# Windowed attention in a two-layer decoder trunk: scores of one head over its own 64 rows, and bias, maximum and sink in one VectorE instruction

## The chip, the cores and the metric

The kernel runs on one core of one Trainium2 chip. The metric is the time of one execution on the device, in microseconds (us), as the median of several runs; the runs before the change gave 1440.52 to 1442.91 us, median 1440.92. A profile of one execution comes with it. In it PE is TensorE's matrix multiplication, PEld its weight load, DVE is VectorE, ACT is ScalarE, POOL is GpSimd and SP is SyncE, which issues most of the DMAs.

## The reference: what is computed

The program is a small decoder trunk over 512 tokens of width 1024, with two layers. Layer one mixes the tokens by a gated delta rule, layer two by causal attention in a sliding window of 128 tokens; each is followed by a gated MLP with a short convolution. The change touches the attention alone:

```python
SWA_Q_HEADS = 16
SWA_KV_HEADS = 4
SWA_HEAD_DIM = 64
SWA_WINDOW = 128
SWA_BLOCK = 128

def sliding_window_sink_attention(hn, k, v, w_q, sinks, w_o, bias, mask):
    bsz, t, _ = hn.shape
    nb = t // SWA_BLOCK
    q = (hn @ w_q).reshape(bsz, nb, SWA_BLOCK, SWA_KV_HEADS, SWA_GROUP, SWA_HEAD_DIM)
    q = q * (SWA_HEAD_DIM ** -0.5)
    ...
    kb, vb = band(k), band(v)
    s = jnp.einsum('bnqhgd,bnkhd->bnhgqk', q, kb).astype(jnp.float32) + bias
    s = jnp.where(mask[None, :, None, None], s, NEG_INF)
    sink = sinks.astype(jnp.float32).reshape(SWA_KV_HEADS, SWA_GROUP)[:, :, None]
    m = jnp.maximum(jnp.max(s, axis=-1), sink)
    p = jnp.exp(s - m[..., None])
    denom = jnp.sum(p, axis=-1) + jnp.exp(sink - m)
    probs = (p / denom[..., None]).astype(vb.dtype)
    o = jnp.einsum('bnhgqk,bnkhd->bnqhgd', probs, vb)
    return o.reshape(bsz, t, SWA_Q_HEADS * SWA_HEAD_DIM) @ w_o
```

`band` gives each block of 128 queries its own 128 keys and the 128 before them (block 0 has only its own). There are 16 query heads of 64 features and 4 heads of keys and values, so four query heads share one key head. `bias` depends only on the distance of query and key, `sinks` holds one number per head.

## The kernel before

The program runs one stage after another: the delta rule, its output projection, `ffn(0)`, `attention`, `ffn(1)`. Activations lie with features on the 128 partitions and the 512 tokens along the free dimension; the residual stream `hT` is eight tiles of 128x512. A product of full accuracy is made of three products in a shorter float format: both operands are split into a high and a low part, and high by high, high by low and low by high are added up. `mm3` (lines 145 to 147) does this for a projection: 8 tiles of weights by 3 products, 24 matmuls of 512 columns into one bank `d`; `cast` (lines 129 and 130) splits the weights, the high part on ScalarE, the low one on VectorE; `split` (lines 150 and 151) does the same for activations.

`attention` normalises `hT`, projects keys and values once (`w_kv`), and then goes through the 16 query heads in eight pairs, `p` = 0 to 7. A pair fills 128 partitions: head `j` = 0 on partitions 0 to 63, head `j` = 1 on 64 to 127. Both heads of a pair use the same key head `g = p // 2`. `query(p)` loads the pair's bias rows and projects its queries; it is called two pairs ahead. `attend(p)` works through four blocks `n` of 128 queries. For a block:

- Lines 1161 to 1163: three score products over all 128 rows. So that the heads stay apart, the keys stand in `kbh` and `kbl` as two halves of 512 columns each: half `j` has the keys on head `j`'s 64 rows and zeros on the other 64. One product gives the scores of both heads, 2 x 256 columns (2 x 128 in block 0), in one bank of tag `s`. There are two such banks.
- Lines 1166 to 1171, VectorE: the bias is added while the scores leave the bank for a row `e` of tag `dt`, the maximum over each head's keys is taken, the sink is brought in (`ngm`, the negative maximum), and the sink's exponent is formed.
- Lines 1172 to 1176: exponentials on ScalarE, which also sums them (`den`); the sum and its reciprocal on VectorE.
- Lines 1178 to 1181: scaling by the reciprocal, head 0 on VectorE, head 1 on ScalarE.
- Lines 1186 to 1197: four transposes on TensorE into a bank of tag `g` (two banks), a copy to the row `pT` on ScalarE, and the product with the values, 64 output partitions for each head, into the bank `p`.

At the end of a pair the bank `p` is split into high and low part, which the output projection over `w_o` reads.

The order of instructions on each engine is set before the run by a scheduler that follows the program's order as priority and puts instructions of other parts where it expects an engine to wait. So projections for later queries stand between the scores and the transposes of a pair. On the chip each engine works through its own list in that order, held by semaphores.

Of the kernel before, what the change touches and what calls it, by code (L numbers as in the profile page):

```python
# [8 lines left out]
F32 = mybir.dt.float32  # L9
# [3 lines left out]
ALU = mybir.AluOpType  # L13
# [28 lines left out]
def kernel(  # L42
# [1059 lines left out]
    def attention(h):  # L1102
        toep = rb[:]
        kbh = [wide("G") for g in range(4)]
        kbl = [wide("L") for g in range(4)]
        for a, b in zip(kbh, kbl):
            for t in (a, b):
                G.memset(t[0:64, 1, :].bitcast(F32), 0.0)
                G.memset(t[64:128, 0, :].bitcast(F32), 0.0)
        kxh, kxl = normed(h, NKV)  # L1110
        rs = rstd_rows(h)
        for kv in range(2):
            st = load_stage(w_kv, 0, 8, 256 * kv)
            for i in range(2):
# [4 lines left out]
                if kv == 0:  # L1119
                    for j in range(2):  # L1120
                        g = 2 * i + j
                        src = f[64 * j : 64 * j + 64, :]
                        near, far = (slice(0, 64), slice(64, 128)) if j == 0 else (slice(64, 128), slice(0, 64))
                        hn_, hf_ = kbh[g][near, j, :], kbh[g][far, 1 - j, :]
                        S.copy(hn_, src)
                        S.copy(hf_, src)
                        V.tensor_tensor(kbl[g][near, j, :], src, hn_.bitcast(F32), op=ALU.subtract)
                        V.tensor_tensor(kbl[g][far, 1 - j, :], src, hn_.bitcast(F32), op=ALU.subtract)
# [22 lines left out]

        def attend(p, qh, ql, b3):
            g = p // 2
            po = bank("p")
            for n in range(NC):
                ns = slice(n * P, (n + 1) * P)
                k0 = max(n - 1, 0) * P
                W = (n + 1) * P - k0
                sc = bank("s")
                s3 = sc[:, 0 : 2 * W].rearrange("p (j k) -> p j k", j=2)  # L1160
                PE.matmul(s3, qh[:, ns], kbh[g][:, :, k0 : k0 + W], start=True, stop=False)
                PE.matmul(s3, qh[:, ns], kbl[g][:, :, k0 : k0 + W], start=False, stop=False)
                PE.matmul(s3, ql[:, ns], kbh[g][:, :, k0 : k0 + W], start=False, stop=True)
                e = r2("ga")
                e3 = e[:, 0 : 2 * W].rearrange("p (j k) -> p j k", j=2)
                V.tensor_tensor(e3, s3, b3[:, :, W - 1 :: -1], op=ALU.add)
                sm = cp.tile([P, 8], F32, tag="sm", bufs=6, name=nm("sm"))
                mx, ngm, den, es = sm[:, 0:2], sm[:, 2:4], sm[:, 4:6], sm[:, 6:8]
                V.tensor_reduce(mx, e3, axis=AX.X, op=ALU.max)
                V.scalar_tensor_tensor(ngm, mx, -1.0, nsink[:, 2 * p : 2 * p + 2], op0=ALU.mult, op1=ALU.min)  # L1170
                V.tensor_tensor(es, sink[:, 2 * p : 2 * p + 2], ngm, op=ALU.add)
                S.activation(es, es, AF.Exp)
                for j in range(2):
                    S.activation(e3[:, j, :], e3[:, j, :], AF.Exp, bias=ngm[:, j : j + 1], accum_out=den[:, j : j + 1])  # L1174
                V.tensor_tensor(den, den, es, op=ALU.add)
                V.reciprocal(den, den)
                for j in range(2):
                    if j == 1:
                        S.activation(e3[:, j, :], e3[:, j, :], AF.Copy, scale=den[:, j : j + 1])
                    else:  # L1180
                        V.tensor_scalar(e3[:, j, :], e3[:, j, :], den[:, j : j + 1], None, op0=ALU.mult)
                pt = bank("g")
                nt = 2 * W // P
                for b in range(nt):
                    bs = slice(b * P, (b + 1) * P)
                    PE.transpose(pt[:, bs], e[:, bs], ident[:])  # L1186
# [89 lines left out]
```

## Time and profile before

| | value |
|---|---|
| median of three runs | 1440.92 us |
| the profiled execution: its own time | 1439.8 us |
| its span, first to last instruction | 1438.0 us |
| mean granted TensorE clock | 0.996 |
| key and value projections, TensorE | from about 897 us |
| first score matmul to last value product | 934 to 1032 us |
| matmul records of scores (L1161 to L1163) | 96 |
| records of transposes (L1186) | 112 |
| records of value products (L1191), two for each matmul | 224 |

The profile names work by line, engine, operation and tiles as `out<-in`, with the buffer numbers left out. A mean in nanoseconds is the duration of one instruction. Matmuls are pipelined: a record's duration holds the way through the array, and the distance from one start to the next tells what a matmul keeps from its successors. "128\*64" behind a matmul is the part of the array that it uses, rows by columns. The idle time in brackets behind a row names what the engine waited for.

### The profile page before, as it was taken

Reading aid. Unit: us, or ns where it says so; the run is one execution under the profiler, and the core shown is the slowest. Engines: PE = TensorE matmul, PEld = TensorE weight load, DVE = VectorE, ACT = ScalarE, POOL = GpSimd, SP = SyncE. Lnnn points to the kernel's source line nnn. Section 1 sums busy time; section 2 is a strip of 40 time slices with the busy share of each in tenths; the row PEclk is TensorE's granted clock in tenths of the full one; section 3 lists DMA queues with packets and bytes.
Section 4 is the critical chain, followed back from the end, with each engine's and each line's share of the span. In section 5 each row is a group of like instructions: output and inputs, shape, how many; then the busy total and the mean of one; then the engine's idle time right before and its main releaser. Section 6 shows DMA issues by size and latency. Waiting matters only on the chain.

```text
span 1438.0 us, 21635 instructions
## 1 busy us (share of the span) xinstructions
PE 1401.4 (97%) x8266; PEld 1165.2 (81%) x8266; DVE 1120.6 (78%) x2056; ACT 770.8 (54%) x1518; POOL 20.0 (1%) x47
## 2 busy tenths in 40 slices
PE   7999999999999999999999999999999999999998
PEld 5777878878876888888988888777788888988887
DVE  5896887979764538889968889787757888977896
ACT  7764666666555434444335445588745444344443
POOL 1000000000000000000000002000000000000000
PEclk9999999999999999999999999999999999999999
DMA  5334254264367323321333223311132322332222
GB/s 156 88 106 114 78 174 121 76 182 125 103 220 227 125 88 110 104 74 53 123 124 111 74 81 111 111 59 45 59 108 90 118 81 66 112 123 88 96 70 77
DMA packets 163084, 152.85 MB, mean 106 GB/s; under 512 B 24164, under 2 KB 150693, under 8 KB 162981
## 3 DMA queue, kind: packets, MB, share of 16 engines
q1 hardware_dynamic: 160722, 151.27, 33.3%
q8 instruction: 65, 1.06, 0.3%
q10 hardware_dynamic: 2259, 0.20, 0.2%
q14 instruction: 38, 0.31, 0.1%
HBM read 134.65 MB, written 16.80 MB: 105 GB/s over the span
## 4 chain that ended last, share of the span: by engine, by line
PE 83%; DVE 8%; DMA 6%; ACT 2%; issue 1%; SPq 0%; DVEq 0%; ACTq 0%
PE d L145 21%; PE d L147 20%; PE d L146 20%; DVE wlo L130 2%; PE s L588 1%; PE p L1191 1%; DMA ol<-od 1%; PE d L992 1%; PE g L1186 1%; PE s L603 1%; PE s L628 1%; PE d L990 1%; PE s L992 1%; PE d L991 1%; DMA stage<-in_a_w_in_dram 1%
## 5 line engine op out<-in xcount | busy, mean ns | idle before, releaser
L145 PE MATMUL d<-xh,whi 128*128 128x512 f32 x1192 | 475.2, 400 | 2.9 <-ACT whi L129 2.8
L146 PE MATMUL d<-xl,whi 128*128 128x512 f32 x1192 | 472.8, 398 | 0.0
L147 PE MATMUL d<-xh,wlo 128*128 128x512 f32 x1192 | 472.0, 398 | 0.7 <-DVE wlo L130 0.7
L129 ACT CAST whi<-stage 128x1024 fp32r<-128x1024 f32 (+2 forms) x236 | 229.1, 976 | 230.3 <-PE d L146 153.9
L130 DVE TENSOR_TENSOR wlo<-stage,whi 128x1024 fp32r<-128x1024 f32 (+2 forms) x236 | 265.5, 1129 | 69.2 <-ACT whi L129 68.6
L145 PEld LDWEIGHTS d<-xh,whi 128*128 128x128 f32 x1192 | 224.6, 188 | 51.2 <-ACT whi L129 3.4
L147 PEld LDWEIGHTS d<-xh,wlo 128*128 128x128 f32 x1192 | 224.3, 188 | 51.5 <-DVE wlo L130 2.1
L146 PEld LDWEIGHTS d<-xl,whi 128*128 128x128 f32 x1192 | 224.3, 188 | 46.2 <-issue 1.0
L237 DVE SCALAR_TENSOR_TENSOR acc<-d,cwc,acc 128x511 f32<-128x511 f32 (+2 forms) x96 | 70.7, 739 | 8.3 <-ACT acc L234 7.9
L851 DVE TENSOR_TENSOR sz<-d,p6s 128x512 f32<-128x512 f32 x58 | 39.9, 689 | 40.9 <-PE d L147 38.4
L873 ACT ACTIVATE dt<-dt 128x512 f32<-128x512 f32 x44 | 27.8, 632 | 81.7 <-DVE dt L856 81.7
L856 DVE SCALAR_TENSOR_TENSOR va<-sz,fcw,va 128x511 f32<-128x511 f32 (+1 forms) x58 | 43.4, 747 | 1.8 <-ACT va L854 0.9
L856 DVE SCALAR_TENSOR_TENSOR dt<-sz,fcw,dt 128x511 f32<-128x511 f32 (+1 forms) x58 | 43.3, 746 | 0.9
L511 DVE TENSOR_TENSOR p6s<-sN,sT 64x31 f32<-64x31 f32 (+15 forms) x124 | 40.7, 328 | 2.5 <-DMA sN<-nd 0.5
L517 DVE TENSOR_TENSOR sT<-sT,p6s 64x31 f32<-64x31 f32 (+15 forms) x124 | 41.0, 330 | 1.9
L129 ACT CAST whi<-st 128x768 fp32r<-128x768 f32 (+1 forms) x30 | 23.7, 791 | 30.5 <-DMA st<-in_ffn_w_down_dram 5.6
L851 DVE TENSOR_TENSOR zl<-d,p6s 128x512 f32<-128x512 f32 x30 | 20.7, 689 | 24.0 <-PE d L147 23.3
L636 ACT ACTIVATE rq<-o 128x128 f32<-128x128 f32 x64 | 19.0, 298 | 28.4 <-DVE o L631 15.8
L1174 ACT ACTIVATE dt<-dt,sm 128x256 f32<-128x256 f32 (+1 forms) x64 | 30.3, 474 | 6.7 <-DVE sm L1170 6.6
L875 DVE TENSOR_TENSOR va<-dt,va 128x512 f32<-128x512 f32 x44 | 30.4, 691 | 1.2
L130 DVE TENSOR_TENSOR wlo<-st,whi 128x768 fp32r<-128x768 f32 (+1 forms) x30 | 26.8, 898 | 1.9 <-ACT whi L129 1.8
L854 ACT ACTIVATE dt<-sz,normc,fcw 128x512 f32<-128x512 f32 x29 | 23.7, 817 | 5.2 <-DVE sz L851 5.1
(745 smaller groups left out, 2796.5 us busy)
## 6 DMA issues: line engine op xcount, KB each, us to landing
stage<-in_ffn_w_up_dram SPq DMA_DIRECT2D x44, 1024.0 KB, 5.2
stage<-in_a_w_in_dram SPq DMA_DIRECT2D x23, 1024.0 KB, 5.8
stage<-in_ffn_w_down_dram SPq DMA_DIRECT2D x16, 768.0 KB, 4.7
stage<-in_a_w_out_dram SPq DMA_DIRECT2D x8, 1024.0 KB, 5.5
st<-in_ffn_w_down_dram SPq DMA_DIRECT2D x8, 768.0 KB, 5.8
zd<-sz SPq DMA_DIRECT2D x16, 256.0 KB, 2.0
od<-o SPq DMA_DIRECT2D x16, 256.0 KB, 2.5
stage<-in_b_w_q_dram SPq DMA_DIRECT2D x4, 1024.0 KB, 5.0
```

The source lines that it names most:

```text
L129: S.copy(hi[:, :kt, :m], src)
L130: V.tensor_tensor(lo[:, :kt, :m], src, hi[:, :kt, :m].bitcast(F32), op=ALU.subtract)
L145: PE.matmul(ps, hi[:, k, :m], xh[k], start=first and k == 0, stop=False)
L146: PE.matmul(ps, hi[:, k, :m], xl[k][:], start=False, stop=False)
L147: PE.matmul(ps, lo[:, k, :m], xh[k], start=False, stop=last and k == kt - 1)
L237: V.scalar_tensor_tensor(acc[:, d:], ps[:, : T - d], col, acc[:, d:], op0=ALU.mult, op1=ALU.add)
L511: V.tensor_tensor(tv, N[:, s, s + 1 : 32].unsqueeze(2).to_broadcast([64, n, m]), Tm[:, s : s + 1, 0:m].to_broadcast([64, n, m]), op=ALU.mult,)
L517: V.tensor_tensor(Tm[:, s + 1 : 32, 0:m], Tm[:, s + 1 : 32, 0:m], tv, op=ALU.subtract)
L851: V.tensor_tensor(u[:], ps[:], rs[:], op=ALU.mult)
L856: V.scalar_tensor_tensor(acc[:, d:], u[:, : T - d], tap(2 - d, t), acc[:, d:], op0=ALU.mult, op1=ALU.add)
L875: V.tensor_tensor(b[:], a[:], b[:], op=ALU.mult)
L1174: S.activation(e3[:, j, :], e3[:, j, :], AF.Exp, bias=ngm[:, j : j + 1], accum_out=den[:, j : j + 1])
```

## The change

The keys of a head are stored twice, once on each half of the partitions, and without zeros: `keys[g]` holds the high part in its first 512 columns and the low part in its second. A score product takes 64 rows of queries and 64 rows of keys, so each head has its own matmul; the matmuls are written with the heads in turn, head 0 into one bank of tag `s`, head 1 into the other. Two blocks are worked on together: both banks of `s` belong to a group of two blocks, each bank with up to 2 x 256 columns of one head.

One VectorE instruction (line 1174) adds the bias, multiplies by -1 and forms the minimum over the keys, beginning from the negative sink; it leaves the negated scores in `e` and the negative maximum in `ngm`. In the list of instructions it stands as two, the operation and the read of its accumulator. The exponential then runs with a scale of -1. The sink's exponent, the sum and the reciprocal run once for a group, over four columns. VectorE does all the scalings. The 16 zero fills on GpSimd are gone.

```diff
-        kbh = [wide("G") for g in range(4)]
-        kbl = [wide("L") for g in range(4)]
-        for a, b in zip(kbh, kbl):
-            for t in (a, b):
-                G.memset(t[0:64, 1, :].bitcast(F32), 0.0)
-                G.memset(t[64:128, 0, :].bitcast(F32), 0.0)
+
+        keys = [wide("G") for g in range(4)]
...
-                        hn_, hf_ = kbh[g][near, j, :], kbh[g][far, 1 - j, :]
-                        S.copy(hn_, src)
-                        S.copy(hf_, src)
-                        V.tensor_tensor(kbl[g][near, j, :], src, hn_.bitcast(F32), op=ALU.subtract)
-                        V.tensor_tensor(kbl[g][far, 1 - j, :], src, hn_.bitcast(F32), op=ALU.subtract)
+                        near, far = [slice(64 * u, 64 * u + 64) for u in (j, 1 - j)]
+                        src, hi = f[near, :], keys[g][near, 0, :]
+                        S.copy(hi, src)
+                        S.copy(keys[g][far, 0, :], src)
+                        V.tensor_tensor(keys[g][near, 1, :], src, hi.bitcast(F32), op=ALU.subtract)
+                        V.tensor_tensor(keys[g][far, 1, :], src, hi.bitcast(F32), op=ALU.subtract)
...
-                PE.matmul(s3, qh[:, ns], kbh[g][:, :, k0 : k0 + W], start=True, stop=False)
-                PE.matmul(s3, qh[:, ns], kbl[g][:, :, k0 : k0 + W], start=False, stop=False)
-                PE.matmul(s3, ql[:, ns], kbh[g][:, :, k0 : k0 + W], start=False, stop=True)
...
+                sc = [bank("s") for j in range(2)]
+                part = lambda j, n, W: sc[j][:, 256 * (n % 2) : 256 * (n % 2) + W]
+                for n, ns, k0, W in blocks:
+                    for i, (q, k) in enumerate(((qh, kh), (qh, kl), (ql, kh))):
+                        for j, hs in enumerate(head):
+                            PE.matmul(
+                                part(j, n, W), q[hs, ns], k[hs, k0 : k0 + W], start=i == 0, stop=i == 2
+                            )
...
+                        V.tensor_tensor_reduce(
+                            out=e[n][:, j * W : j * W + W],
+                            in0=part(j, n, W),
+                            in1=b3[:, j, W - 1 :: -1],
+                            scale=-1.0,
+                            scalar=nsink[:, 2 * p + j : 2 * p + j + 1],
+                            op0=ALU.add,
+                            op1=ALU.min,
+                            accum_out=ngm[:, u : u + 1],
+                        )
...
+                        S.activation(
+                            ej, ej, AF.Exp, bias=ngm[:, u : u + 1], scale=-1.0, accum_out=den[:, u : u + 1]
+                        )
...
-                    if j == 1:
-                        S.activation(e3[:, j, :], e3[:, j, :], AF.Copy, scale=den[:, j : j + 1])
-                    else:
-                        V.tensor_scalar(e3[:, j, :], e3[:, j, :], den[:, j : j + 1], None, op0=ALU.mult)
+                        V.tensor_scalar(ej, ej, den[:, u : u + 1], None, op0=ALU.mult)
```

Three places show how the order moves. In the rows the text ahead of `<-` is what is written and the text behind it what is read, with the tile's number; `qT` holds the keys, `rq` and `S` the high and low queries, `d` a projection, `g` a bank of transposes, `p` a bank of value products. First TensorE before, in the fourth pair, where scores of single blocks stand between transposes and value products:

```order
L1161 MATMUL s_9204<-qT_8371,rq_9023 128x512
L1162 MATMUL s_9204<-sy_8375,rq_9023 128x512
L1186 MATMUL g_9069<-ident_80,dt_9056 128x128 x2
L1163 MATMUL s_9204<-qT_8371,S_9024 128x512
L145 MATMUL d_9292<-xh_8619,whi_9293 128x512
L146 MATMUL d_9292<-xl_8620,whi_9293 128x512
L1186 MATMUL g_9069<-ident_80,dt_9056 128x128 x2
L1186 MATMUL g_9097<-ident_80,dt_9084 128x128 x4
L1161 MATMUL s_9232<-qT_8371,rq_9023 128x512
```

The same engine in the changed kernel, the second group of the third pair; `s_9055` is the bank of head 0, `s_9056` that of head 1:

```order
L147 MATMUL d_9118<-xh_8603,wlo_9120 128x512
L1165 MATMUL s_9055<-qT_8371,rq_8853 128x256 x2
L1165 MATMUL s_9055<-qT_8371,S_8854 128x256
L1165 MATMUL s_9056<-qT_8371,rq_8853 128x256 x2
L1165 MATMUL s_9056<-qT_8371,S_8854 128x256
L1165 MATMUL s_9055<-qT_8371,rq_8853 128x256
L1165 MATMUL s_9056<-qT_8371,rq_8853 128x256
L1165 MATMUL s_9055<-qT_8371,rq_8853 128x256
L1165 MATMUL s_9056<-qT_8371,rq_8853 128x256
L1165 MATMUL s_9055<-qT_8371,S_8854 128x256
L1165 MATMUL s_9056<-qT_8371,S_8854 128x256
L145 MATMUL d_9118<-xh_8607,whi_9119 128x512
```

A group's twelve score matmuls now stand together, and in this group the first block's three products of head 0 come ahead of its three of head 1; only the second block has the heads in turn. In the first group of a pair all six pairs are in turn.

Second, VectorE before, where the instructions of several blocks are mixed (`s_8932` and `s_8960` below belong to different blocks, and a block's maximum does not wait for another block's sum):

```order
L1170 SCALAR_TENSOR_TENSOR sm_8910<-sm_8910,nsink_381 128x2
L1166 TENSOR_TENSOR dt_8936<-s_8932,sz_8690 128x512
L1171 TENSOR_TENSOR sm_8910<-sink_380,sm_8910 128x2
L1169 TENSOR_REDUCE sm_8938<-dt_8936 128x2
L1175 TENSOR_TENSOR sm_8886<-sm_8886 128x2
L1166 TENSOR_TENSOR dt_8964<-s_8960,sz_8690 128x512
L1176 RECIPROCAL sm_8886<-sm_8886 128x2
```

VectorE in the changed kernel, second pair, from the end of its first group to the second group's new instructions (`ISA` is the new operation, the row with `sm` alone the read of its accumulator):

```order
L1185 TENSOR_TENSOR sm_8872<-sink_380,sm_8872 128x4
L1196 TENSOR_TENSOR sm_8872<-sm_8872 128x4
L1197 RECIPROCAL sm_8872<-sm_8872 128x4
L1202 TENSOR_SCALAR dt_8873<-dt_8873,sm_8872 128x128 x2
L1202 TENSOR_SCALAR dt_8874<-dt_8874,sm_8872 128x256 x2
L1174 ISA dt_8924,sm_8923<-s_8909,sz_8670,nsink_381 128x256
L1174 ISA sm_8923 128x1
L1174 ISA dt_8924,sm_8923<-s_8910,sz_8670,nsink_381 128x256
L1174 ISA sm_8923 128x1
```

From the second pair on, a group's first instructions on VectorE stand behind the whole of the group ahead of it.

76 lines of the change are left out of this document (41 added, 35 removed).

## The prediction

> **What bounds the kernel now.** I read the page's busy times and its chain of waits first, then the stage that the change touches, then single rows of that stage.
>
> ```profile
> PE 1401.4 (97%) x8266; PEld 1165.2 (81%) x8266; DVE 1120.6 (78%) x2056; ACT 770.8 (54%) x1518; POOL 20.0 (1%) x47
> ...
> PE 83%; DVE 8%; DMA 6%; ACT 2%; issue 1%; SPq 0%; DVEq 0%; ACTq 0%
> ```
>
> TensorE is busy in 97% of the span and 83% of the chain that ended last runs through it. The first score matmul of the attention starts at 934 us and its last value product ends at 1032 us. One row of the busy times by stretch covers that stage (columns: TensorE, weight load, VectorE, ScalarE, GpSimd, granted clock, DMA).
>
> ```profile
> 934.00:1033.00 99.00, 99.00 (x625) 72.73 (x624) 76.62 (x252) 79.11 (x247) 0.00 (x0) 1.00 0.17 51
> ```
>
> TensorE has no gap in these 99 us at full clock; VectorE and ScalarE have over 20 us each to spare. What the stage is worth is therefore the sum of TensorE's steps, 99 / 8 = 12.4 us for each of the eight pairs of heads. VectorE or ScalarE work counts only where TensorE comes to wait for it. The busy time does not show what a step costs, since matmuls overlap; the start-to-start distance does. Rows in order of time, with start and duration in us:
>
> ```profile
> 933.90 0.39 PE L146 MATMUL d<-xl,whi 128*128 128x512 f32 x1
> 934.13 0.40 PE L147 MATMUL d<-xh,wlo 128*128 128x512 f32 x1
> 934.37 0.28 PE L1161 MATMUL s<-kT,rq 128*128 128x256 f32 x1
> 934.48 0.27 PE L1162 MATMUL s<-sy,rq 128*128 128x256 f32 x1
> ...
> 934.71 0.40 PE L1161 MATMUL s<-kT,rq 128*128 128x512 f32 x1
> 934.95 0.40 PE L1162 MATMUL s<-sy,rq 128*128 128x512 f32 x1
> 935.18 0.39 PE L1163 MATMUL s<-kT,S 128*128 128x512 f32 x1
> ```
>
> A matmul over 512 columns takes a step of 0.235 us, one over 256 columns 0.117 us (934.37 to 934.71 is three of them). The half of the keys that is zero costs as much as the half that is used.
>
> **The change, part 1: the score matmuls.** Removed for each pair of heads: nine of 512 columns and three of 256 (block 0). For eight pairs that is 72 x 0.235 + 24 x 0.117 = 19.7 us. Added for each pair: 18 of 256 columns and 6 of 128 columns, each over 64 rows, 192 in all. Whether two that use different rows run side by side decides their cost. No row of before has such a pair in this number format; the nearest are small products over 32 rows each, which lie on different rows and columns:
>
> ```profile
> 131.90 0.19 PE L542 MATMUL s<-Xg,nt 32*32 32x32 f32 x1
> 131.90 0.19 PE L541 MATMUL s<-Xg,nt 32*32 32x32 f32 x1
> 131.93 0.19 PE L542 MATMUL s<-Xg,nt 32*32 32x32 f32 x1
> 131.94 0.19 PE L541 MATMUL s<-Xg,nt 32*32 32x32 f32 x1
> ```
>
> The two start together and the next two 0.03 us later. So TensorE does run two small tiles at once, and I take it that two 64-row products of 256 columns share one step of 0.117 us. For those of 128 columns the bounds are 0.06 us (half of the 256-column step) and 0.117 us; no row of this format has a step under 0.115, so I take 0.117.
>
> Matmuls start in program order, so the order counts. In the first group of a pair (blocks 0 and 1) the heads alternate: six steps. In the second group (blocks 2 and 3) three products of head 0 stand ahead of three of head 1, and only the rest alternate. Then the first three of head 0 take steps 1 to 3, those of head 1 steps 3 to 5, and the rest end in step 8. That makes 8 x (6 + 8) = 112 steps x 0.117 = 13.1 us, a gain of 6.6 us. If nothing overlaps, 192 steps cost 22.5 us, a loss of 2.8.
>
> **Part 2: changes of tile.** A product over 64 rows uses the array in another division than its neighbours, as the value products (128\*64) do already:
>
> ```profile
> 949.68 0.40 PE L147 MATMUL d<-xh,wlo 128*128 128x512 f32 x1
> 950.01 0.66 PE L1191 MATMUL p<-acc,Vp 128*64 128x128 f32 x8
> 950.60 0.50 PE L145 MATMUL d<-xh,whi 128*128 128x512 f32 x1
> 950.94 0.39 PE L146 MATMUL d<-xl,whi 128*128 128x512 f32 x1
> ```
>
> From 949.68 to 950.01 is 0.33 us in place of 0.235: the next division waits until the last product is nearly through, about 0.1 us for each change. Counted in the order of instructions from the first score matmul to the last value product, before has 62 such changes (all around the value products) and the changed kernel 87, because each group of scores is now entered and left as well, while two blocks share more of their neighbours. 25 x 0.1 = 2.5 us lost. The bounds are 0 and 0.2 us for one.
>
> **Part 3: VectorE and ScalarE.** Grouped rows of the stage (count, busy us, mean ns):
>
> ```profile
> L1169 DVE TENSOR_REDUCE sm<-dt 128x2 f32<-128x512 f32 x24 | 16.3, 680 | 0.1
> L1166 DVE TENSOR_TENSOR dt<-s,sz 128x512 f32<-128x512 f32 x18 | 12.3, 683 | 1.4 <-PE g L1186 1.1 <-ACT dt L1179 0.3
> L130 DVE TENSOR_TENSOR wlo<-stage,whi 128x1024 fp32r<-128x1024 f32 x7 | 8.5, 1218 | 1.9 <-ACT whi L129 1.9
> L1181 DVE TENSOR_SCALAR dt<-dt,sm 128x256 f32<-128x256 f32 x24 | 8.4, 348 | 0.3
> L1176 DVE RECIPROCAL sm<-sm 128x2 f32<-128x2 f32 x32 | 5.1, 158 | 0.3
> ...
> L1147 DVE SCALAR_TENSOR_TENSOR va<-d,p6s 128x512 f32<-128x512 f32 x7 | 4.8, 690 | 5.6 <-PE d L147 5.6
> L151 DVE TENSOR_TENSOR S<-va,rq 128x512 fp32r<-128x512 f32 x7 | 4.8, 679 | 0.0
> ...
> L1169 DVE TENSOR_REDUCE sm<-dt 128x2 f32<-128x256 f32 x8 | 3.3, 412 | 0.0
> L1166 DVE TENSOR_TENSOR dt<-s,sz 128x256 f32<-128x256 f32 x6 | 2.5, 418 | 1.0 <-PE s L1163 0.8 <-PE g L1186 0.2
> L1181 DVE TENSOR_SCALAR dt<-dt,sm 128x128 f32<-128x128 f32 x8 | 2.2, 279 | 0.0
> ```
>
> The new instruction and the read of its running minimum do not occur before. The lower bound for both over 256 columns is the plain add, 0.42 us; the upper one is add and maximum apart, 0.42 + 0.41 = 0.83. I take the add and one small instruction, 0.42 + 0.16 = 0.57, since the add's row is the same operands with one more operation behind it; over 128 columns 0.28 + 0.16 = 0.43. Per pair of heads: before 3 x (0.68 + 0.68 + 4 x 0.16 + 0.35) + 0.42 + 0.41 + 4 x 0.16 + 0.28 = 8.8 us; after 6 x 0.57 + 2 x 0.43 + 6 x 0.16 + 6 x 0.35 + 2 x 0.28 = 7.9 us. VectorE loses 7 us in the stage although it takes over all the scaling.
>
> ```profile
> L1179 ACT ACTIVATE dt<-dt,sm 128x256 f32<-128x256 f32 x24 | 12.1, 508 | 0.2 <-DVE sm L1176 0.2
> ...
> L1172 ACT ACTIVATE sm<-sm 128x2 f32<-128x2 f32 x32 | 6.1, 195 | 0.8 <-DVE sm L1171 0.6
> ```
>
> ScalarE loses the scalings (over 12.1 us) and half of the 32 sink exponentials (3 us). Neither is on the path: both lie beside TensorE's 99 us, and I cost them at nothing.
>
> What could uncover them is the order on VectorE. From the second pair of heads on, the new instructions of the second group stand behind the first group's sum, reciprocal and scalings, and those wait for ScalarE's last exponential. Its price by rows:
>
> ```profile
> 954.27 0.49 ACT L1174 ACTIVATE dt<-dt,sm 128x256 f32<-128x256 f32 x1
> 954.67 0.18 ACT L1174 ACTIVATION_READ_ACCUMULATOR dt<-dt,sm 128x1 f32 x1
> ...
> 954.89 0.16 DVE L1175 TENSOR_TENSOR sm<-sm 128x2 f32<-128x2 f32 x1 [1.32 <-ACT dt L1174]
> 955.09 0.17 DVE L1176 RECIPROCAL sm<-sm 128x2 f32<-128x2 f32 x1
> ...
> 955.29 0.35 DVE L1181 TENSOR_SCALAR dt<-dt,sm 128x256 f32<-128x256 f32 x1
> ...
> 986.71 0.68 DVE L1166 TENSOR_TENSOR dt<-s,sz 128x512 f32<-128x512 f32 x1
> 987.31 0.15 DVE L1170 SCALAR_TENSOR_TENSOR sm<-sm,nsink 128x2 f32<-128x2 f32 x1
> ```
>
> From the last exponential to the sum 0.62 us, to the first scaling 1.02; and without a wait an instruction starts about 0.08 us before the last one's end (986.71 to 987.31 is 0.60). So VectorE's own loop per pair is 6 x 0.41 + 2 x 0.27 for the eight new instructions with their reads, 2 x 1.1 for the two waits and small sums, 6 x 0.27 + 2 x 0.2 for the scalings, and 0.61 + 1.14 + 2 x 0.6 for the query's evacuation, the weight split and the two splits: 10.2 us. TensorE's loop is 12.4 - 4.1 / 8 = 11.9 us. The cover is 1.7 us per pair. The single bank per head asks for no more: four new instructions take some 1.5 us, and in seven of the eight pairs six to eleven projections of 0.235 us (1.4 to 2.6 us) stand between the first group's scores and the next. At the short end waits of some 0.3 us for the transposes may appear in every other pair, about 1 us; the score waits that are halved give as much back. I take nothing for both.
>
> **Part 4: keys.** The 16 zero fills leave GpSimd.
>
> ```profile
> 896.66 0.52 POOL L1109 MEMSET qT<- 64x512 f32 x1
> ...
> 910.98 0.62 ACT L1125 CAST kT<-va 64x512 fp32r<-64x512 f32 x1 [0.76 <-DVE va L1118]
> ```
>
> The last ends 14 us ahead of the first copy into the keys, which waits for VectorE: nothing. Copies and splits of the keys stay in number and size. On SP one w_o load moves ahead of one bias row, which is not needed until pairs later: nothing. In the last MLP some splits on VectorE move by one turn, beside other projections: nothing, and 1 us either way in the range.
>
> **Sum.** 6.6 - 2.5 = 4.1 us less than the profiled execution's 1439.8 us (span 1438.0 and 1.8 around it): 1435.7. The median shown is 1440.92, 1.1 above that execution, so I predict **1436.8 us**.
>
> **The rivals.**
> - *No overlap* (the other side, slower): products over different rows run one after the other in this format. Then 2.8 + 2.5 = 5.3 us are lost: 1446.2. It decides where a pair's step is over (19.7 - 2.5) / 112 = 0.154 us. For it: the two products write the same 128 partitions of two banks, which no row of before does. Against it: the rows at 131.90. Chance 0.18.
> - *Half an overlap*: a pair's step of about 0.15 us, because both write at once into the same partitions; gain and tile changes cancel: 1440.8. Chance 0.12. The Trainium skill, "TensorE: Matmul & The Clock Gate", section "Measured speedup vs the span model", measured 3.07 times for four row tiles, not four times; an estimate from it for two tiles is a step of 0.15 us and a sum of about zero. No run here shows it yet.
> - *VectorE becomes the bound*: the new instruction costs its upper bound of 0.83 us. Then VectorE's loop is 10.2 + 8 x 0.26 = 12.3 us against 11.9, so 8 x 0.4 = 3.2 us are given back: 1440.0. It decides from 0.78 us on. Chance 0.15.
> - *TensorE's waits go too*: fewer waits for ScalarE and VectorE in front of transposes and value products, some 20 of 0.1 us: 1434.8. Chance 0.10.
>
> **How the numbers follow.** The forecast has 0.45, with a range of its own of 1434.3 to 1439.3 from the bounds on tile changes; with 128-column steps of 0.06 us its low end is 1433.0. A measurement tells 0.2%, 2.9 us, from no change, so faster means under 1438.0 and slower over 1443.8. Faster: 0.32 of the forecast's 0.45, all 0.10 of the last rival and 0.03 of the VectorE case, 0.45. Slower: 0.17 of no overlap, 0.04 of a dearer VectorE and 0.02 of half an overlap, 0.23. The rest, 0.32, is the same. The range runs from that low end to the price of no overlap, 1433.0 to 1446.5.
>
> **What would show it.** Score products of two heads that start within 0.02 us of each other and 0.117 us after the last two show part 1 right; starts 0.117 us apart for every one show the first rival. About 0.1 us before and after each group of scores shows part 2. The new VectorE instruction near 0.42 us with a short read behind it, and no rows in which a transpose or a score's weight load waits long for VectorE, show part 3. The prediction is wrong if the stage's 98 us do not shorten by about 4, or if the time comes from any other stage.

## The result and the profile after

The changed kernel takes 1464.78 us (median of four runs, 1463.91 to 1465.58) against 1441.28 for the kernel before: 23.5 us slower, ratio 1.0161 with a 95% interval of 1.0144 to 1.0179. The forecast was 1436.8. Of the executions below one, of before_up64, took 4781.05 us where its three others took 1452 to 1454; its ratio leaves it out, and the cause is not known.

The page's busy times and the shares of its chain of waits, of the changed kernel:

```profile
PE 1420.4 (97%) x8362; PEld 1171.7 (80%) x8362; DVE 1115.5 (76%) x2072; ACT 757.6 (52%) x1470; POOL 11.7 (1%) x31
...
PE 81%; DVE 8%; DMA 5%; ACT 4%; issue 1%; SPq 0%; DVEq 0%; ACTq 0%
```

TensorE is still 97% busy and VectorE and ScalarE are busy for less than before (1115.5 for 1120.6, 757.6 for 770.8). A page like this doesn't show where 25 us of span (1463.2 for 1438.0) went. The stage does, in part (busy time by stretch, first score product to last value product):

```profile
945.00:1049.00 104.00, 98.44 (x704) 70.24 (x704) 70.36 (x268) 64.60 (x199) 0.00 (x0) 1.00 0.15 48
```

It takes 103.6 us instead of 97.9, and TensorE, which had no gap, now has 5.6 us of them. The stage also holds 14 projection products fewer than before (174 for 188), so for the same work it is some 9 us longer. But it begins at 945.0 instead of 934.4, ahead of anything that the change touches. I matched every matmul outside the attention with its twin in the trace before: in the long projections the distance grows by some 0.3 us in every 20 us, from 5.5 us at 460 to 9.8 us at 820, and again behind the attention. One stretch of pure projections, in the second MLP, first before, then after:

```profile
1100.00:1190.00 90.00, 90.00 (x395) 73.85 (x394) 74.76 (x108) 41.91 (x58) 0.00 (x0) 1.00 0.29 94
```

```profile
1100.00:1190.00 90.00, 90.00 (x389) 72.97 (x388) 73.84 (x107) 43.31 (x60) 0.00 (x0) 1.00 0.30 97
```

In the same 90 us, at the same granted clock (1.00) and with TensorE busy throughout, 389 products start instead of 395. Start to start, a 512-column product takes 232.4 ns on average where it took 229.0. The duration column hides this (0.39 us in both): only counts, or distances of starts, show it. So there are two losses, one in every projection of the program and one in the attention.

For the attention, TensorE's rows in a pair of heads (start and duration in us, in brackets a wait):

```profile
958.20 0.44 PE L1165 MATMUL s<-kT,rq 64*128 64x128 f32 x4
958.48 0.27 PE L1165 MATMUL s<-kT,S 64*128 64x128 f32 x2
958.58 0.45 PE L1165 MATMUL s<-kT,rq 64*128 64x256 f32 x4
958.87 0.28 PE L1165 MATMUL s<-kT,S 64*128 64x256 f32 x2
959.08 0.50 PE L145 MATMUL d<-xh,whi 128*128 128x512 f32 x1
...
961.51 0.40 PE L146 MATMUL d<-xl,whi 128*128 128x512 f32 x1
962.33 0.50 PE L1165 MATMUL s<-kT,rq 64*128 64x256 f32 x2 [0.42 <-DVE sm L1174]
...
963.63 0.49 PE L147 MATMUL d<-xh,wlo 128*128 128x512 f32 x1
964.47 0.30 PE L1207 MATMUL g<-ident,dt 128*128 128x128 f32 x1 [0.34 <-DVE dt L1202]
```

The first group's twelve score products take 0.88 us (958.20 to 959.08), in pairs, as forecast. The second group waits for VectorE: 0.82 us pass after a projection that needs 0.23, then the first transpose comes 0.84 us after another. VectorE at that time:

```profile
958.30 0.69 DVE L1142 SCALAR_TENSOR_TENSOR va<-d,p6s 128x512 f32<-128x512 f32 x1 [3.66 <-PE d L147]
958.91 0.68 DVE L151 TENSOR_TENSOR sy<-p,sy 128x512 fp32r<-128x512 f32 x1
959.51 1.22 DVE L130 TENSOR_TENSOR wlo<-stage,whi 128x1024 fp32r<-128x1024 f32 x1
960.64 0.69 DVE L151 TENSOR_TENSOR S<-va,rq 128x512 fp32r<-128x512 f32 x1
961.25 0.34 DVE L1174 CUSTOM_DVE_ANT_0 dt<-s,sz,nsink 128x128 f32<-128x128 f32 x1
961.51 0.08 DVE L1174 DVE_READ_ACCUMULATOR2_ANT sm<- 128x1 f32 x1
...
962.19 0.48 DVE L1174 CUSTOM_DVE_ANT_0 dt<-s,sz,nsink 128x256 f32<-128x256 f32 x1
```

The scores were complete by about 959.1. The four reductions (`CUSTOM_DVE_ANT_0` and its read) start at 961.25, because the evacuation of a query, the split of the last pair's result, a weight subtraction for the projection of a later pair and the query's split stand ahead of them in VectorE's list. VectorE had idled for 3.66 us before that, held by the evacuation at the head of its list.

### The profile page after: what moved, and what is told of

Read it like the earlier page. It is cut to its first block, busy times and chain, and to the rows that moved or that the text cites. A ratio compares the mean times of both kernels' runs of the same rounds, so it can differ in the third digit from the quotient of the medians.

```text
span 1463.2 us, 21769 instructions
## 1 busy us (share of the span) xinstructions
PE 1420.4 (97%) x8362; PEld 1171.7 (80%) x8362; DVE 1115.5 (76%) x2072; ACT 757.6 (52%) x1470; POOL 11.7 (1%) x31
## 4 chain that ended last, share of the span: by engine, by line
PE 81%; DVE 8%; DMA 5%; ACT 4%; issue 1%; SPq 0%; DVEq 0%; ACTq 0%
PE d L147 20%; PE d L145 20%; PE d L146 20%; DVE wlo L130 2%; PE s L588 1%; PE p L1212 1%; DMA stage<-in_ffn_w_down_dram 1%; PE d L992 1%; PE s L603 1%; ACT dt L1193 1%; PE s L628 1%; PE d L990 1%; PE s L992 1%; DMA ol<-od 1%; PE d L991 1%
## 5 line engine op out<-in xcount | busy, mean ns | idle before, releaser
L129 ACT CAST whi<-stage 128x1024 fp32r<-128x1024 f32 (+2 forms) x236 | 229.2, 976 | 250.3 <-PE d L146 172.0
L130 DVE TENSOR_TENSOR wlo<-stage,whi 128x1024 fp32r<-128x1024 f32 (+2 forms) x236 | 265.6, 1129 | 66.5 <-ACT whi L129 65.3
L130 DVE TENSOR_TENSOR wlo<-st,whi 128x768 fp32r<-128x768 f32 (+1 forms) x30 | 26.8, 899 | 1.8 <-ACT whi L129 1.7
```

Of the source, the lines that this page charges most:

```text
L129: S.copy(hi[:, :kt, :m], src)
L130: V.tensor_tensor(lo[:, :kt, :m], src, hi[:, :kt, :m].bitcast(F32), op=ALU.subtract)
```

## The experiments

The place of the tiles was the suspect for the first loss. The small tile `sm` lies ahead of the big tiles in memory. It had 6 buffers of 32 bytes and now has 4 of 48, each padded to 64: the big tiles start 64 bytes higher. Before, every activation tile started 32 bytes past a multiple of 256 (288 past one of 2048), now 96; the split weights start at 224 in both.

**before_up64.** The kernel before, moved up by 64 unused bytes in `cp`, the pool that lies ahead of the big tiles' pool `main`.

```diff
+    cp.tile([P, 16], F32, name="pad")
     ffn(0, hT)
     attention(hT)
```

> The kernel before with 64 unused bytes per partition ahead of the big tiles, so that every activation tile starts 64 bytes higher (352 in place of 288 bytes past a multiple of 2048), as it does in the changed kernel; nothing else moves. Theory 'place': the step of a 512-column projection goes from 229.0 to 232.4 ns in all stages and the time to 1456 us (1453 to 1459), the attention's 98 us staying without gaps. Rival 'program' (the longer step comes from the changed instructions, whatever the addresses): step 229.0 ns, time 1441 us.

1453.63 us against 1440.68, ratio 1.0086 (1.0069 to 1.0103), with 387 products in the 90 us:

```profile
1100.00:1190.00 90.00, 90.00 (x387) 72.48 (x386) 73.07 (x104) 40.95 (x56) 0.00 (x0) 1.00 0.29 94
```

Sixty-four unused bytes cost 13 us; the attention keeps its length (98.05 us).

**after_home.** The changed kernel, moved back: `sm` goes to the end of `main`, and 192 unused bytes take the room that it had in `cp` before.

```diff
-                sm = cp.tile([P, 12], F32, tag="sm", bufs=4, name=nm("sm"))
+                sm = main.tile([P, 12], F32, tag="sm", bufs=4, name=nm("sm"))
...
+    cp.tile([P, 48], F32, name="pad")
```

> The changed kernel with the activation tiles back at the addresses of before (its small tile sm put at the end of the big tiles instead of ahead of them). Theory 'place': steps of 229.0 ns again outside the attention, time 1449 us (1446 to 1452); the attention keeps its waits and is 8 to 9 us longer than before. Rival 'program': steps 232.4 ns, time 1465 us.

1451.75 us, ratio to before 1.0074 (1.0057 to 1.0091); the same 90 us have 395 products again:

```profile
1100.00:1190.00 90.00, 90.00 (x395) 73.94 (x394) 73.62 (x105) 41.85 (x57) 0.00 (x0) 1.00 0.29 94
```

So 13.0 us of the loss are the place, from both sides. The other 10.5 to 11 us are the change itself. In this profile matching products stand 3.1 us late ahead of the attention, within what executions of one kernel differ, and 12.1 behind it: 9.0 in the stage.

**steps_by_start, steps_by_start2, steps_by_start3.** Nothing but products of 512 columns, by the start of the operands; the rest of the program is left out, and the output is zeros. The loop for one start:

```diff
+    for r in range(36):
+        PE.matmul(ps_[:], wt[:, 0 + 128 * (r % 8) : 0 + 128 * (r % 8) + 128], mv[:, 56 : 56 + 512], start=r == 0, stop=r == 35)
```

> No attention and no trunk: 36 products of 512 columns in a row from one tile, for 16 starts of the moving operand (0 to 1024 bytes past a multiple of 2048), first beside casts, subtractions and weight loads on the other engines, then alone; the output is zeros. Theory 'place': the step depends on the start alone, about 229 ns at 288 and 232.4 ns at 352, with other engines or without. Rival 'contention': the step is the same for all starts when alone and differs only in company. Rival 'program': no difference at all.

TensorE's rows of steps_by_start, the part with no other engine at work, for starts of 224, 256, 288, 320, 352 and 416 bytes, 36 products each:

```profile
205.84 8.35 PE L211 MATMUL ps<-mv,wt 128*128 128x512 f32 x36
214.03 8.56 PE L216 MATMUL ps<-mv,wt 128*128 128x512 f32 x36
222.43 8.41 PE L221 MATMUL ps<-mv,wt 128*128 128x512 f32 x36
230.68 8.57 PE L226 MATMUL ps<-mv,wt 128*128 128x512 f32 x36
239.09 8.56 PE L231 MATMUL ps<-mv,wt 128*128 128x512 f32 x36
247.49 8.56 PE L236 MATMUL ps<-mv,wt 128*128 128x512 f32 x36
```

From one row to the next, divided by 36: 227.5 ns at 224, 233.3 at 256, 229.2 at 288 and 233.3 at 352. In company of the other engines (the rows of this run up to 89 us) the numbers are the same within 0.4 ns. All 16 starts: 229 at 32 and 288, 227 at 224 and 480, over 233 at the rest, so the pattern repeats after 256 bytes. The weights stood at 224.

> No attention and no trunk: 24 products of 512 columns for each of 8 starts of the weights (0 to 224 bytes past a multiple of 256) with each of 8 starts of the moving operand; the output is zeros. Theory 'moving': the step depends on the moving operand's start alone, 227.3 at 224, 229 at 32, 233 at the others. Theory 'together': it depends on where weights and moving operand start relative to each other (0 and 64 bytes apart in the first row of starts), so the fast ones move along the diagonal.

This run told nothing: TensorE needed 0.82 us and later 0.60 us for each product throughout, with no other engine at work. The cause is open. The traces of the three steps_by_start runs hold no record of the granted clock (their pages have no PEclk row, and the 1.0 beside their span is no measurement), so a slower clock isn't excluded.

> As steps_by_start2 (8 starts of the weights by 8 of the moving operand, 16 products each), with casts, subtractions and weight loads on the other engines as in the first row of starts. Theory 'moving': the columns for 32 and 224 are fast (229 and 227 ns) in every row of weights. Theory 'together': the fast ones move with the weights' start.

Rows of steps_by_start3 with the weights at 128 and the moving operand at 128, 160, 192 and 224, 16 products each:

```profile
147.24 3.81 PE L275 MATMUL ps<-mv,wt 128*128 128x512 f32 x16
150.89 3.90 PE L280 MATMUL ps<-mv,wt 128*128 128x512 f32 x16
154.62 3.83 PE L285 MATMUL ps<-mv,wt 128*128 128x512 f32 x16
158.29 3.90 PE L290 MATMUL ps<-mv,wt 128*128 128x512 f32 x16
162.03 3.90 PE L295 MATMUL ps<-mv,wt 128*128 128x512 f32 x16
```

The last row is the next start and ends the fourth. 228.1 ns where both start alike (128), 229.4 where the moving operand starts 64 bytes further than the weights (192), over 233 for the other two. In all eight rows of weights, but for the first sixteen products, in which TensorE starts up, the fast ones lie on these two diagonals (227 to 228 and 229 to 230 ns), and all others take 232 to 234: 'together' holds. Before, the moving operand started 64 bytes further than the weights, modulo 256 (32 against 224); in the changed kernel 128 (96 against 224).

**before_up192.** The kernel before with both operands at 224: `cp.tile([P, 48], F32, name="pad")`.

> The kernel before with 192 unused bytes ahead of the big tiles, so that they start 224 bytes past a multiple of 256. Theory 'place', with the period of 256 bytes that the row of starts showed: the projection's step falls from 229.0 to 227.3 ns; by the ratio of the run 64 bytes up (12.9 us for 4 ns) the time falls by 5 us, to 1435.5 (1433 to 1438). Rival (the step of 229 in the kernel has another cause than in the row of starts): no change, 1441.

1437.51 us, ratio 0.9973 (0.9964 to 0.9983); 398 products in the 90 us. This is the fastest version of the study, faster than both kernels.

```profile
1100.00:1190.00 90.00, 90.00 (x398) 74.52 (x398) 75.71 (x109) 43.01 (x59) 0.00 (x0) 1.00 0.31 99
```

All further kernels stand at the addresses of before.

**ttr_only.** The one VectorE instruction alone, in the kernel before.

```diff
-                V.tensor_tensor(e3, s3, b3[:, :, W - 1 :: -1], op=ALU.add)
-                V.tensor_reduce(mx, e3, axis=AX.X, op=ALU.max)
-                V.scalar_tensor_tensor(ngm, mx, -1.0, nsink[:, 2 * p : 2 * p + 2], op0=ALU.mult, op1=ALU.min)
...
+                for j in range(2):
+                    V.tensor_tensor_reduce(out=e3[:, j, :], in0=s3[:, j, :], in1=b3[:, j, W - 1 :: -1], scale=-1.0,
+                        scalar=nsink[:, 2 * p + j : 2 * p + j + 1], op0=ALU.add, op1=ALU.min, accum_out=ngm[:, j : j + 1])
...
```

> The kernel before with one part of the change: bias, maximum and sink in one VectorE instruction per head and block; scores, keys, block order and scaling as before. Theory: the instruction takes 0.48 us and VectorE's saving lies beside a TensorE that has no gap, so 1441 us, within 3 us. Rival 'instruction': the new instruction itself holds up others, and some of the loss of 23.5 us shows here, 1446 us or more.

1440.15 us, ratio 1.0000 (0.9991 to 1.0010). The instruction costs nothing and brings nothing.

**rows128.** The changed kernel (groups of two blocks, one instruction, all scaling on VectorE) with the old products: 96 over 128 rows, a bank for each block.

```diff
-                            PE.matmul(part(j, n, W), q[hs, ns], k[hs, k0 : k0 + W], start=i == 0, stop=i == 2)
...
+                    PE.matmul(s3, qh[:, ns], kbh[g][:, :, ks], start=True, stop=False)
+                    PE.matmul(s3, qh[:, ns], kbl[g][:, :, ks], start=False, stop=False)
+                    PE.matmul(s3, ql[:, ns], kbh[g][:, :, ks], start=False, stop=True)
```

> The changed kernel at the addresses of before, with the old score products: zero-padded keys, 128 rows, one bank per block, but still two blocks as a group, with the one VectorE instruction and the common sums. Tile changes fall from 87 to 48 (before: 62). Theory 'grouping' (the loss of 11 us against before comes from TensorE waiting for a group's maxima and scalings): the waits of about 10 us stay, 1.4 us of tile changes go, so 1449 us (1446 to 1453), with waits in front of transposes of the same size. Rival 'tiles' (products over 64 rows and the changes of tile cost more than counted): the time is that of before, 1441 us.

1440.48 us, ratio 0.9999 (0.9989 to 1.0008). My theory 'grouping' fell: the loss needs the new score products. VectorE's rows at the same place as above:

```profile
946.17 0.69 DVE L151 TENSOR_TENSOR sy<-p,sy 128x512 fp32r<-128x512 f32 x1 [3.52 <-ACT sy L150]
946.78 0.68 DVE L1148 SCALAR_TENSOR_TENSOR va<-d,p6s 128x512 f32<-128x512 f32 x1
947.38 0.34 DVE L1179 CUSTOM_DVE_ANT_0 dt<-s,sz,nsink 128x128 f32<-128x128 f32 x1
...
950.21 1.22 DVE L130 TENSOR_TENSOR wlo<-stage,whi 128x1024 fp32r<-128x1024 f32 x1
```

Here the reductions come straight behind the evacuation and the weight subtraction behind six of them. I did not see then that this was the difference.

**sums_apart.** Each block with its own sum, reciprocal and scaling: `sm`, `e` and all that follows moved into a loop over the two blocks.

> The changed kernel at the addresses of before, scores still two blocks at a time in two banks, but each block with its own sink exponent, sum, reciprocal and scaling, ordered block by block. Tile changes rise from 87 to 104 (1.7 us). Theory 'grouping', in the form that the common sums of four columns hold the first block's transposes back: the six waits of 0.6 us in front of transposes go and some more, 1451.75 - 4 to 6 + 1.7 = 1448 us (1446 to 1450). Rival 'banks' (the first wait is for both banks to come free, sums do not matter): 1452 to 1454.

1453.24 us, ratio 1.0086 (1.0071 to 1.0101): no sign that the common sums are to blame, though 17 more changes of tile (1.7 us, as expected above) could hide a small gain.

**rows128_heads.** As rows128, but head 0 of both blocks in one bank and head 1 in the other: `PE.matmul(part(j, n, W), q[:, ns], k[g][:, j, k0 : k0 + W], ...)` for each head.

> As rows128 (zero-padded keys, 128 rows, two blocks as a group), but the scores of head 0 of both blocks go to one bank and those of head 1 to the other, as in the changed kernel: 192 products that cannot overlap, 50 changes of tile instead of 87. Theory 'banks' (a bank per head is held by both blocks of a group, so the next group's products wait for all four maxima, and its transposes for what follows): waits of about 0.8 us in front of scores and transposes as in the changed kernel, 1451 us (1448 to 1455). Rival 'tiles' (products over 64 rows, with their changes of tile, cost the 11 us): 1441 us, as rows128.

1449.88 us, ratio 1.0066 (1.0051 to 1.0081). So the loss comes without any product over 64 rows. That looked like a proof of 'banks', but the run had changed two things: the banks, and the number of products.

**halves.** One block at a time, heads in two banks that are kept for a pair, their halves in turn.

```diff
+            sc = [bank("s") for j in range(2)]
+            for n in range(NC):
...
+                        PE.matmul(sc[j][:, 256 * (n % 2) : 256 * (n % 2) + W], q[hs, ns], k[hs, k0 : k0 + W], ...)
```

> The changed kernel with one block at a time: own rows, heads in two banks, but the two banks kept for a whole pair of heads and their halves of 256 columns used in turn, and sums for each block. The next block's products wait only for the maxima two blocks back. Tile changes rise to 166 against 87 (7.9 us); only one block in two overlaps its heads. Theory 'banks': the long waits in front of scores and transposes go (8 to 10 us), so about 1451 us, with rows of waits over 0.5 us gone. Rival 'tiles': 1451.75 + 8 = 1460 us.

1465.07 us, ratio 1.0169 (1.0154 to 1.0184): both theories missed, the first by more. TensorE enters the 64-row division 59 times instead of 23, and the time from a score product to the next product, summed over all 192, rises from 19.1 to 29.5 us.

**banks3.** `BANKS = {"d": 2, "g": 2, "s": 3, "p": 1}`.

> The changed kernel at the addresses of before with three banks for scores and two for projections in place of two and three. A group's first head finds a free bank while the group ahead is still reduced. Theory 'banks': the waits in front of the second group's scores and its transposes shrink, and the attention loses 3 to 8 of its 9 us; the other stages may lose by the missing projection bank (unknown, read stage by stage). Rival 'tiles': the attention stays 9 us longer than before.

1495.14 us, ratio 1.0381 (1.0364 to 1.0399). 36 us are lost ahead of the attention (its first score product at 970.8 instead of 934.4), which itself loses 16: the missing projection bank drowns what was to be seen. Inconclusive.

**scale_split.** Head 1's scaling back on ScalarE: `S.activation(ej, ej, AF.Copy, scale=den[:, u : u + 1])`.

> The changed kernel at the addresses of before with head 1's scaling back on ScalarE. Theory 'banks': the waits in front of transposes end with the scalings, but ScalarE's take 0.5 us against 0.35, so within 2 us of 1451.75. Rival 'scaling' (VectorE, which does all the scaling, is what is waited for): 3 us or more faster.

1449.28 us, ratio 1.0058 (1.0043 to 1.0073), 2.5 below after_home with intervals that overlap: between the two expectations. By matching products, as above, the stage of its one profile is 5.4 us longer than before, where after_home's is 9.0. So the scalings, which on VectorE stand ahead of the next group's reductions, may be worth up to 3.6 us; one profile does not settle it.

**rows128_split.** As rows128, a bank per block, with each head's products by themselves: 192 as in rows128_heads.

> As rows128 (a bank per block), but each head's products by themselves, 192 of 128 or 256 columns as in rows128_heads: only the banks differ from that run. Theory 'banks': most of the 9.4 us between rows128 and rows128_heads is the bank per head that both blocks hold, so this is 1443 us (1441 to 1445), the surplus being the products of 128 columns that cost a step of about 0.11 us like those of 256 (24 x 0.11 = 2.7 us). Rival 'products' (192 small products cost more than 96 large ones, whatever the bank): 1449 us.

1451.03 us, ratio 1.0071 (1.0050 to 1.0092). 'Banks' fell; the 192 products cost 10.5 us against rows128 whatever the bank. The waits of TensorE in the attention, first of rows128, then of rows128_split (us in total, times, longest):

```profile
PE p L1217 <- ACT acc L1214: 0.2, 1, 0.2
```

```profile
PE s L1170 <- DVE sm L1179: 3.3, 6, 0.6
PE g L1212 <- DVE dt L1207: 0.6, 1, 0.6
PE p L1217 <- ACT ol L1214: 0.4, 1, 0.4
```

The scores' own time rises too, from 20.6 to 25.0 us: a product of 128 columns takes a step of 0.11 us like one of 256, and there are 48 of them instead of 24 of 256. The rest is waiting, and in this kernel too the subtraction (L130) and a query's split stand ahead of the reductions.

**rows128_major.** Head 0's reductions of both blocks first (the two loops exchanged).

> As rows128_heads (a bank per head), but VectorE reduces head 0 of both blocks first and then head 1, so that head 0's bank comes free two instructions earlier (about 0.9 us). Theory 'banks': the next group's first products start earlier and the waits in front of them shrink, 1446 us (1444 to 1448). Rival 'products': as rows128_heads, 1450 us. Against the theory would also be a longer time by the later first block, 1451 us or more: then what counts is the time at which a block's exponentials can begin.

1449.17 us, ratio 1.0057 (1.0035 to 1.0079), as rows128_heads: again not the banks.

**weights_later, split_later.** Nothing but VectorE's order: the subtraction is issued behind the first four reductions of a pair, in after_home and in rows128_split.

```diff
-            mm3(ps[:], cast(stq[p // 2], 8, p % 2), KD, qxh, qxl)
+            if p < 4:
+                w = cast(stq[p // 2], 8, p % 2)
+            else:
+                with tc.issue_after(first[p - 4]):
+                    w = cast(stq[p // 2], 8, p % 2)
+            mm3(ps[:], w, KD, qxh, qxl)
```

`first` holds the last reduction of each pair's first group; the output projection's weights are treated alike.

> The changed kernel at the addresses of before; only VectorE's order differs: the weight subtraction of a later projection (1.22 us), which stood ahead of each pair's first four reductions, is issued behind them. Same instructions, same banks. Theory 'order' (the reductions stand behind other work on VectorE, and TensorE waits for them): in seven pairs the reductions start 1.1 us earlier and the waits of 0.83 us in front of the second group's scores and of the transposes shrink, 1446 us (1443 to 1448.5). Rival 'products' (192 small products with their visits to another tile cost the rest): 1451 to 1452 us as after_home.

> The same one change of order in rows128_split (192 products over 128 rows, a bank per block), where the weight subtraction stood ahead of the reductions too, though not in rows128. Theory 'order': most of the 10 us between rows128 and rows128_split go, up to the 2.7 us that the products of 128 columns cost, 1444 us (1442 to 1447). Rival 'products': 1451 us.

split_later: 1446.79 us (1446.03 to 1449.04) against 1451.03 (1450.51 to 1454.70) for rows128_split, ratio to before 1.0045 (1.0030 to 1.0060). No execution of one lies among those of the other, and by matching products the stage loses 5.5 us against before instead of 9.5. The order of one instruction per pair is worth about 4 us. Its waits, same columns, where rows128_split had 3.3 us in front of scores and 0.6 in front of transposes:

```profile
PE s L1175 <- DVE sm L1184: 1.5, 7, 0.2
```

weights_later: 1449.90 us, ratio 1.0064 (1.0045 to 1.0083), 1.9 below after_home with intervals that overlap. The transposes' waits in front of scalings fall from 2.6 us to 0.6, as 'order' said, but those in front of scores rise from 2.2 to 3.3:

```profile
PE s L1170 <- DVE sm L1179: 3.3, 6, 0.7
PE g L1214 <- DVE dt L1209: 0.6, 2, 0.4
PE p L1219 <- ACT acc L1216: 0.3, 1, 0.3
```

In the stage, as against before, 6.5 us remain of 9.0. Here the subtraction, where it now stands, comes ahead of the second group's reductions. VectorE in the second pair:

```profile
954.18 0.48 DVE L1179 CUSTOM_DVE_ANT_0 dt<-s,sz,nsink 128x256 f32<-128x256 f32 x1
954.59 0.08 DVE L1179 DVE_READ_ACCUMULATOR2_ANT sm<- 128x1 f32 x1
954.59 1.22 DVE L130 TENSOR_TENSOR wlo<-stage,whi 128x1024 fp32r<-128x1024 f32 x1
955.73 0.16 DVE L1192 TENSOR_TENSOR sm<-sink,sm 128x4 f32<-128x4 f32 x1
955.80 0.48 DVE L1179 CUSTOM_DVE_ANT_0 dt<-s,sz,nsink 128x256 f32<-128x256 f32 x1
```

The subtraction is one of three or four instructions ahead of the reductions; to move the others was not tried, and 1446 was not reached.

## Why the prediction was wrong

**The step that failed first was none of its steps.** Its sum took every projection outside the attention as unchanged ("or if the time comes from any other stage" stood only among the things that would make it wrong). The 1,192 rows of one projection line on the changed kernel's page, times three lines, times 3.4 ns, are 12.2 us:

```profile
L145 PE MATMUL d<-xh,whi 128*128 128x512 f32 x1192 | 478.3, 402 | 2.9 <-ACT whi L129 2.8
```

The measured price was 13.0. The cause is one line of the change, which the excerpt in "The change" does not show: `sm` goes from `[P, 8]`, `bufs=6` to `[P, 12]`, `bufs=4`. No part of the prediction asked what a changed tile size moves.

**Part 1 (scores).** Right in its mechanism: two heads' products share a step, and 128 columns cost about as much as 256. The size was off. In the rows at 958.20 three pairs of 128 columns take 0.38 us (0.127 each) and the first two pairs of 256 columns 0.29 (0.145 each): the second pair of a block starts 0.17 us behind the first, later ones 0.11. So the step is some 0.13 us on average, not 0.117. It lies between the forecast and the 0.15 that the prediction estimated from the Trainium skill, "TensorE: Matmul & The Clock Gate", section "Measured speedup vs the span model". The groups in which the heads don't alternate take 1.30 us, not 8 x 0.117 + 0.1 = 1.04: the first product of such a group holds the second for 0.22 us instead of 0.12. Products and 23 exits of 0.1 were to take 13.1 + 2.3 = 15.4 us and take 19.1; the old scores with theirs took 22.4, so 3.3 us are saved. 'No overlap' is out: rows128_heads, the same 192 products over all rows, spends 25.0 us on them.

**Part 2 (changes of tile).** Right: 0.32 us from the last projection to the first score product at 957.88 to 958.20, and about 0.2 us from the last score product to the next projection, each some 0.1 above the plain step.

**Part 3 (VectorE).** The prices were right or high: 0.48 us for 256 columns, 0.34 for 128, the next starting 0.41 and 0.27 later with the read between. VectorE did not become the bound, and rows128 and ttr_only show that all its new work costs nothing. The cover failed. "The cover is 1.7 us per pair" and "The single bank per head asks for no more ... I take nothing for both" compared sums of two engines per pair. But what the next group's scores wait for is not VectorE's sum. It is the place of the four reductions in its list: 2.3 us of other work stood ahead of them (958.91 to 961.25), and they themselves take 1.4. From the first group's end to the second group's first product 3.25 us pass (959.08 to 962.33); six to eleven projections of 0.23 us, 1.4 to 2.6 us, don't cover that. I read the added order on TensorE and counted projections there, and did not read what stood ahead of the reductions on VectorE. The term taken as nothing, with the smaller gain of part 1, made the attention 9 us longer instead of 4 shorter.

Part of it is shown: split_later gives 4.2 us back by order alone, and rows128, with the reductions in front, has no such waits. In weights_later's profile the order gives 2.5 of the stage's 9.0 us, but its executions overlap with after_home's. Where the 9 us lie, the starts in the profiles tell. Against rows128 after_home loses 4.6 us between projections and the transposes that follow them, 4.1 between projections and the score products that follow them (15 changes of tile of 0.1 are in it) and 1.6 from projection to projection, and gains 1.6 in the scores' own time. How much of these waits is order alone is not settled. Nor is it shown why the order set ahead of the run puts other work in front when the products are 192. With 192 in groups of two blocks the subtraction stands ahead of the first reductions in seven of the eight pairs, unless it is moved; in halves it does in three, in rows128 with 96 in one.

**Part 4.** Nothing, as forecast, for keys, zero fills and queues: the stage starts 10.6 us late, of which 7 are the place (before_up64) and 3 stay in after_home, within what executions of one kernel differ.

## What to carry to other kernels

When a change alters the size or number of any buffer, compare the start addresses of everything behind it, and compare the start-to-start step of an untouched stage before explaining the touched one. An engine with 20 us to spare can still hold the one that bounds the kernel: read, in its list, what stands ahead of the instruction that is waited for, since a saving on the bounding engine is lost when its partner answers later. An experiment that moves two things at once (banks and number of products) proves neither.

## What the runs showed of the hardware

- The step of a 512-column product depends on the starts of its two operands relative to each other, modulo 256 bytes (steps_by_start and steps_by_start3, starts in multiples of 32 bytes): 227 to 228 ns when equal, 229 to 230 when the moving operand is 64 bytes further, 232 to 234 otherwise, with other engines at work or not. In the whole kernels, at a granted clock of 1.00 in the 90 us compared, the difference of 3.4 ns is 13 us.
- Two products over 64 rows each, in different banks, start in the changed kernel within 0.02 us of each other and share a step of 0.11 us for 128 or 256 columns, 0.17 behind the first pair of a block. The first two of one head alone are 0.22 us apart.
- Products alone, with no other engine at work, once ran at 0.60 to 0.82 us each for a whole millisecond (steps_by_start2, whose trace has no record of the clock); in steps_by_start, where other engines worked first, they stayed at 0.23 us after these had stopped. Why is open.
